# Eighteen weight pieces of a hybrid decoder block: the subtraction that splits them, on VectorE in place of GpSimd

## The chip, the core and the metric

The kernel runs on one core of a Trainium2 chip. The core's engines work side by side, each with its own queue of instructions in a fixed order: TensorE (PE, matrix products into PSUM), VectorE (DVE), ScalarE (ACT), GpSimd (POOL), and SyncE (SP), which here only starts DMAs. Instructions wait for one another by semaphores. The metric is the time of one execution on the device in microseconds (us), less is better.

## The reference, cut to what matters

One decoder layer on 512 tokens of width 1024. `u` is the normed input; one projection of `u` feeds a gated DeltaNet (GDN: short convolution, a triangular solve per chunk, a recurrence over chunks), a sparse attention (an indexer picks 128 keys per query) and two gates; then the output projection and a gated feed-forward with a short convolution.

```
proj = einsum("bsd,de->bse", u, w_in)          # q,k,v,z,a,b | dq,dk,dv | index q,k,w | gates a,b
gq, gk, gv = split(silu(causal_dwconv(g_qkv, gdn_conv_w)))      # gq, gk normed per head
T = triangular_solve(A + eye, eye)             # A[i,j] = beta_i (k_i . k_j) gamma_ij below the diagonal
u_, w = T @ (v * beta), T @ (k * beta * eG)
v_new = u_ - w @ state;  o = qg @ state + att @ v_new;  state = state * dlast + kd.T @ v_new
o_gdn = rmsnorm(o, gdn_norm_g) * silu(z)
score = sum_h iw[t,h] * relu(iq[t,h] . ik[s]) ; keep the top 128 causal keys ; softmax over them
m = sigmoid(gate_A) * o_gdn + sigmoid(gate_B) * o_dsa
h = h + m @ w_out ;  h = h + (silu(f_gate) * f_val) @ w_down ;  out = rmsnorm(h)
```

## The kernel before, in words

Every weight matrix is cut into pieces of 128 x 1024 numbers, in the order in which they are used. A piece is loaded from DRAM into a tile `raw`, ScalarE rounds it into its high part `whi` (line 198), and the low part `wlo = raw - whi` is a subtraction on an engine that the caller names (line 199, `piece(lo_engine)`). `raw`, `whi` and `wlo` have three buffers each. The activations are split in the same way (`uTh`, `uTl`; `xgh`, `xgl`). A product is then three matmuls (`passes`, lines 206 to 208): low times high, high times low, high times high, added up in a PSUM tile `acc`.

`channel_major` uses two pieces for two PSUM tiles of 128 channels by 512 tokens (48 matmuls of 512 columns); `token_major` uses two pieces for all tokens by 256 channels (96 matmuls of 256 columns). Which engine makes the low part of the first and of the second piece is their argument: `P` is GpSimd, `V` is VectorE.

The order of the work: the small projections; `uTh`/`uTl` (lines 421 to 425, one slice for each of eight blocks of 128 rows of `u`); the indexer's queries; then `gdn_half(0)` on heads 0 to 3: keys, queries and values (`conv_silu`, lines 463 to 469), the blocks `MT` of the solve's matrix (line 543), a round trip through DRAM, the solve itself on VectorE (lines 589 and 591, 30 steps of two dependent instructions with both inputs in SBUF), another round trip, transposes `UT` (line 601), the block inversion on TensorE (from line 607), and the recurrence over four chunks of 128 tokens (lines 637 to 665: `TR`, `upd`, `kS`). Beside it VectorE picks the top keys (lines 694 and 697) and the projections `dk` and `dq` are made (lines 701 to 709). Then `gdn_half(1)`, the attention (32 items, `attend_a` and `attend_b`), the gate projections `z`, `ga`, `gb` in 12 chunks, the mix, the output projection and the feed-forward.

This is the order in which the program is written. The order in which each engine's queue stands is made by a scheduler that runs over the whole program: it takes an instruction as soon as its model of the engines says that it is ready, by a priority that follows the written order, and pieces have their priority raised by 2000 places (line 196). So one stage's matmuls stand between another's small steps, and a change of one engine's work moves instructions on all engines.

Of the kernel before, what the change touches and what calls it, by code (L numbers as in the profile page):

```python
# [86 lines left out]
def hybrid_block(ctx: ExitStack, tc: tile.TileContext, x: bass.AP, xc: bass.AP, wp: bass.AP,  # L87
                 chan: bass.AP, rows: bass.AP, out: bass.AP):
    nc = tc.nc
    V, A, P, T = nc.vector, nc.scalar, nc.gpsimd, nc.tensor  # L90
# [5 lines left out]
    def acc(name="acc"):  # L96
        return psum.tile([128, 512], F, name=name, tag="acc", bufs=3)

    def tp(name="tp"):
        return psum.tile([128, 512], F, name=name, tag="tp", bufs=2)  # L100
# [4 lines left out]
    def rec(name="rec"):  # L105
        return psum.tile([128, 512], F, name=name, tag="rec", bufs=2)
# [87 lines left out]
    def piece(lo_engine):  # L194

        with tc.high_priority(offset=2000):
            raw, hi, lo = load()
            A.copy(hi, raw)  # L198
            lo_engine.tensor_sub(lo, raw, hi.bitcast(F))  # L199
        return hi, lo  # L200

    def passes(o, lhs, rhs, first, last, shared=False):


        (lh, ll), (rh, rl) = lhs, rhs
        a = T.matmul(o, lh, rl, start=first, stop=False, skip_group_check=shared)  # L206
        T.matmul(o, ll, rh, start=False, stop=False, skip_group_check=shared)  # L207
        return a, T.matmul(o, lh, rh, start=False, stop=last, skip_group_check=shared)  # L208

    def cols(pc, k, n, c0, c1):  # L210
        return tuple(w.rearrange("p (k c) -> p k c", c=n)[:, k, c0:c1] for w in pc)
# [81 lines left out]
    def u_blk(k, tb):  # L293
        return uTh[:, k, 128 * tb:128 * tb + 128], uTl[:, k, 128 * tb:128 * tb + 128]

    def token_major(eng):

        pcs = [piece(eng), piece(eng)]
        ps = [acc().rearrange("p (t c) -> p t c", c=256) for _ in range(2)]
        for i in range(2):  # L300
            for tb in range(NT):
                for k in range(4):
                    kk = 4 * i + k
                    passes(ps[tb // 2][:, tb % 2], u_blk(kk, tb), cols(pcs[i], k, 256, 0, 256),
                           kk == 0 and tb % 2 == 0, kk == KT - 1, shared=True)
        return ps

    def channel_major(eng, src=None, second=P):
        pcs = [piece(eng), piece(second)]
        ps = [acc(), acc()]  # L310
        for i, pc in enumerate(pcs):
            for t in range(2):
                for k in range(4):
                    kk = 4 * i + k
                    passes(ps[t], cols(pc, k, 256, 128 * t, 128 * t + 128),
                           src[kk] if src else (uTh[:, kk], uTl[:, kk]), kk == 0, kk == KT - 1)
        return ps
# [4 lines left out]
    def half_kb(name):  # L322
        return PR.tile([128, 512], F, name=name, tag="dqo", bufs=9)
# [119 lines left out]
    for b in range(1, NT):  # L443
        n = 128 * (b + 1)
        score[b] = mask[:, m_off[b]:m_off[b] + n]
        for h in range(H):
            p = tp("rel")[:, :n]
# [12 lines left out]
    def conv_silu(p, ti, dst=None):  # L460
        y = PR.tile([128, 512], F, name="y", bufs=2)
        t = PR.tile([128, 512], F, name="t", bufs=5)
        A.activation(y, p, AF.Identity, scale=cw[:, ti, 3:4])
        for s in range(1, 4):
            V.scalar_tensor_tensor(y[:, s:], p[:, :512 - s], cw[:, ti, 3 - s:4 - s], y[:, s:],  # L465
                                   op0=OP.mult, op1=OP.add)
        A.activation(t, y, AF.Tanh)
        dst = t if dst is None else dst
        V.scalar_tensor_tensor(dst, t, 1.0, y, op0=OP.add, op1=OP.mult)
        return dst  # L470
# [4 lines left out]
    def gdn_half(hh):  # L475
# [23 lines left out]


        for j in range(2):
            for t, p in enumerate(channel_major(P, second=V if hh else P)):
                conv_silu(p, 8 + HH * hh + 2 * j + t, kT[:, 2 * j + t])
        sumsq(kT, ssk, kt)
        V.tensor_scalar(ssk, ssk, EPS, None, op0=OP.add)
# [18 lines left out]
        for c in range(NT):  # L524
# [10 lines left out]
            for h2 in range(2):  # L535
                p = rec("kk").rearrange("p (h a i) -> p h a i", h=2, a=2)
# [145 lines left out]
        oA.append(at)  # L682

    gdn_half(0)


# [3 lines left out]
    for b in range(1, NT):  # L690
        n = 128 * (b + 1)
        top = const.tile([128, 8], F, name="top", bufs=2)
        for i in range(TOPK // 8):
            t = V.max(top, score[b])  # L694
# [4 lines left out]


    dk = PR.tile([128, 2, 512], F, name="dk", tag="k4", bufs=2)
    for t, p in enumerate(channel_major(P)):
        A.copy(dk[:, t], p)
    dq = []
    for j in range(4):
        for t, p in enumerate(channel_major(P)):
            q = half_kb("dq")
            A.copy(q, p)
            dq.append(q)

    gdn_half(1)

    oB = []
# [48 lines left out]
    def gate_bias(off):  # L762
        gb = PR.tile([128, 256], F, name="gbias", bufs=2)
        A.dma_start(gb, bcast(2048 + off, 256))
        return gb.unsqueeze(1).to_broadcast([128, 2, 256])

    def tmp(name):
        return PR.tile([128, 512], F, name=name, tag="t", bufs=5).rearrange("p (t c) -> p t c", c=256)

    def gated(o, p, bias):  # L770
        t = tmp("tg")
        V.tensor_add(t, p, bias)
        A.activation(t, t, AF.Tanh, scale=0.5)
        V.scalar_tensor_tensor(o, t, 1.0, o, op0=OP.add, op1=OP.mult)

    def z_chunk(j):
        for t2, p in enumerate(token_major(P)):
            t = tmp("tz")
            A.activation(t, p, AF.Tanh, scale=0.5)
            V.scalar_tensor_tensor(t, t, 1.0, p, op0=OP.add, op1=OP.mult)  # L780
            o = oAv[j][:, 2 * t2:2 * t2 + 2]
            P.tensor_mul(o, o, t)

    def ga_chunk(j):
        bias = gate_bias(256 * j)
        for t2, p in enumerate(token_major(P)):
            gated(oAv[j][:, 2 * t2:2 * t2 + 2], p, bias)

    def gb_chunk(j):
# [25 lines left out]
    for kind, j in _GATES:  # L815
        {"z": z_chunk, "ga": ga_chunk, "gb": gb_chunk}[kind](j)
        if kind == "gb" and j < 2:
            mix_chunk(j)
        if kind == "ga" and j >= 2:
            mix_chunk(j)  # L820
# [100 lines left out]
    for f in range(NF):  # L921
        e = P if f < 2 else V
# [124 lines left out]
```

## Time and profile before

| what | value |
|---|---|
| median of 3 runs (lowest, highest) | 950.55 us (949.44, 951.9) |
| the profiled execution: its time, and its span from first to last instruction | 950.98 us, 949.2 us |
| busy in the span: PE, DVE, ACT, POOL | 920.1, 601.7, 442.9, 193.3 us |
| mean granted TensorE clock | 0.988 |

The 1.8 us between span and time lie before the first and after the last instruction. A matmul's busy time overlaps the next one's, so a PE that is busy all the time can still be waiting for a moment; how dense its matmuls are is seen from how many start in a stretch. The granted clock has two levels, 1.2 and 2.4 GHz; a share of 1.00 means 2.4 GHz all through a stretch.

### The profile page before, as it was taken

Reading aid. Unit: us, or ns where it says so; the run is one execution under the profiler, and the core shown is the slowest. Engines: PE = TensorE matmul, PEld = TensorE weight load, DVE = VectorE, ACT = ScalarE, POOL = GpSimd, SP = SyncE. Lnnn points to the kernel's source line nnn. Section 1 sums busy time; section 2 is a strip of 40 time slices with the busy share of each in tenths; the row PEclk is TensorE's granted clock in tenths of the full one; section 3 lists DMA queues with packets and bytes.
Section 4 is the critical chain, followed back from the end, with each engine's and each line's share of the span. In section 5 each row is a group of like instructions: output and inputs, shape, how many; then the busy total and the mean of one; then the engine's idle time right before and its main releaser. Section 6 shows DMA issues by size and latency. Waiting matters only on the chain.

```text
span 949.2 us, 14678 instructions
## 1 busy us (share of the span) xinstructions
PE 920.1 (97%) x5671; PEld 807.0 (85%) x5671; DVE 601.7 (63%) x1222; ACT 442.9 (47%) x954; POOL 193.3 (20%) x131
## 2 busy tenths in 40 slices
PE   9989999979999998899999999999999999999997
PEld 8868877868888898899999999888888888888886
DVE  6885999889649769455634546666656665522424
ACT  7547754414559663355544435534444444422213
POOL 0264425411213352222243032000000000000201
PEclk9989999989999999999999999999999999999999
DMA  9323212432211232311422222323223332232212
GB/s 341 103 89 92 87 67 78 134 89 84 73 45 45 79 89 73 74 51 51 158 77 91 88 89 90 112 92 109 88 89 94 107 105 95 88 110 90 89 67 89
DMA packets 39830, 89.30 MB, mean 94 GB/s; under 512 B 15664, under 2 KB 16976, under 8 KB 39760
## 3 DMA queue, kind: packets, MB, share of 16 engines
q1 hardware_dynamic: 24192, 81.91, 25.9%
q10 hardware_dynamic: 15568, 6.45, 2.8%
q8 instruction: 45, 0.74, 0.3%
q14 instruction: 25, 0.20, 0.1%
HBM read 85.18 MB, written 3.16 MB: 93 GB/s over the span
## 4 chain that ended last, share of the span: by engine, by line
PE 72%; DVE 18%; DMA 3%; issue 2%; ACT 2%; POOL 1%; ACTq 0%; DVEq 0%; POOLq 0%
PE acc L206 19%; PE acc L207 18%; PE acc L208 18%; PE d L207 3%; PE d L208 3%; PE d L206 3%; DVE tw L589 2%; DVE wi L591 2%; DVE y L465 2%; PE lg L718 1%; DVE mask L697 1%; PE lg L736 1%; DMA MT<-bl 1%; DVE top L694 1%; DMA nn<-bl 1%
## 5 line engine op out<-in xcount | busy, mean ns | idle before, releaser
L198 ACT CAST whi<-raw 128x1024 fp32r<-128x1024 f32 x136 | 142.5, 1048 | 222.1 <-PE acc L208 102.3
L199 DVE TENSOR_TENSOR wlo<-raw,whi 128x1024 fp32r<-128x1024 f32 x80 | 99.7, 1247 | 158.8 <-ACT whi L198 158.6
L199 POOL TENSOR_TENSOR wlo<-raw,whi 128x1024 fp32r<-128x1024 f32 x56 | 139.0, 2484 | 294.4 <-ACT whi L198 260.3
L207 PE MATMUL acc<-hTh,wlo 128*128 128x512 f32 (+1 forms) x368 | 139.8, 380 | 0.0
L206 PE MATMUL acc<-hTl,whi 128*128 128x512 f32 (+1 forms) x368 | 139.1, 381 | 0.2 <-DVE hTl L845 0.2
L208 PE MATMUL acc<-hTh,whi 128*128 128x512 f32 (+1 forms) x368 | 138.8, 380 | 0.0
L206 PE MATMUL acc<-wlo,uTh 128*128 128x256 f32 x384 | 112.8, 294 | 1.1 <-DVE y L465 1.1
L206 PE MATMUL acc<-uTl,whi 128*128 128x512 f32 x272 | 109.5, 404 | 3.8 <-DVE uTl L425 3.6
L207 PE MATMUL acc<-whi,uTl 128*128 128x256 f32 x384 | 113.2, 295 | 0.0
L208 PE MATMUL acc<-whi,uTh 128*128 128x256 f32 x384 | 112.8, 294 | 0.0
L207 PE MATMUL acc<-uTh,wlo 128*128 128x512 f32 x272 | 108.7, 400 | 0.0
L208 PE MATMUL acc<-uTh,whi 128*128 128x512 f32 x272 | 108.2, 398 | 0.0
L206 PEld LDWEIGHTS acc<-hTl,whi 128*128 128x128 f32 x368 | 69.2, 188 | 13.4 <-DVE hTl L845 0.4
L207 PEld LDWEIGHTS acc<-hTh,wlo 128*128 128x128 f32 x368 | 69.2, 188 | 13.1
L208 PEld LDWEIGHTS acc<-hTh,whi 128*128 128x128 f32 x368 | 69.2, 188 | 13.1
L987 POOL TENSOR_TENSOR h<-h,gf 128x512 f32<-128x512 f32 (+1 forms) x8 | 10.6, 1349 | 338.6 <-ACT sq L983 338.6
L206 PEld LDWEIGHTS acc<-wlo,uTh 128*128 128x128 f32 x384 | 74.3, 194 | 2.8 <-DVE y L465 1.3
L207 PEld LDWEIGHTS acc<-whi,uTl 128*128 128x128 f32 x384 | 74.5, 194 | 1.6 <-issue 1.0
L208 PEld LDWEIGHTS acc<-whi,uTh 128*128 128x128 f32 x384 | 74.4, 194 | 1.6 <-issue 1.2
L904 DVE SCALAR_TENSOR_TENSOR fy<-acc,ch,fy 128x511 f32<-128x511 f32 x88 | 65.7, 747 | 11.0 <-ACT fy L902 9.5
L206 PEld LDWEIGHTS acc<-uTl,whi 128*128 128x128 f32 x272 | 52.1, 192 | 15.2 <-DVE uTl L425 4.7
L208 PEld LDWEIGHTS acc<-uTh,whi 128*128 128x128 f32 x272 | 52.1, 191 | 10.5
(310 smaller groups left out, 1891.1 us busy)
## 6 DMA issues: line engine op xcount, KB each, us to landing
raw<-in_wp_dram SPq DMA_DIRECT2D x137, 512.0 KB, 3.4
xT<-in_xc_dram SPq DMA_DIRECT2D x8, 256.0 KB, 5.2
xt<-in_x_dram SPq DMA_DIRECT2D x4, 512.0 KB, 8.4
ge<-gdr ACTq DMA_DIRECT2D x8, 256.0 KB, 3.2
h<-in_x_dram SPq DMA_DIRECT2D x4, 512.0 KB, 5.8
out_dram<-h SPq DMA_DIRECT2D x8, 256.0 KB, 2.3
raw<-in_wp_dram SPq DMA_DIRECT2D x4, 256.0 KB, 4.7
gbias<-in_rows_dram ACTq DMA_DIRECT2D x8, 128.0 KB, 3.1
```

Of the source, the lines that this page charges most:

```text
L198: A.copy(hi, raw)
L199: lo_engine.tensor_sub(lo, raw, hi.bitcast(F))
L206: a = T.matmul(o, lh, rl, start=first, stop=False, skip_group_check=shared)
L207: T.matmul(o, ll, rh, start=False, stop=False, skip_group_check=shared)
L208: return a, T.matmul(o, lh, rh, start=False, stop=last, skip_group_check=shared)
L465: V.scalar_tensor_tensor(y[:, s:], p[:, :512 - s], cw[:, ti, 3 - s:4 - s], y[:, s:], op0=OP.mult, op1=OP.add)
L589: V.tensor_mul(w, wi[:, 0:c, j:j + 1].to_broadcast([128, c, m]), nn[:, j:j + 1, j + 1:].to_broadcast([128, c, m]))
L591: tri.append(V.tensor_sub(wi[:, 0:c, j + 1:], wi[:, 0:c, j + 1:], w))
L694: t = V.max(top, score[b])
L697: V.match_replace(score[b], top, score[b], TAKEN)
L904: V.scalar_tensor_tensor(y[:, s:], p[:, :512 - s], fw[:, ti, 2 - s:3 - s], y[:, s:], op0=OP.mult, op1=OP.add)
L987: P.tensor_mul(hv, hv, gf[:, 512 * half + c.start:512 * half + c.stop])
```

## The change

The low parts of 18 pieces move from GpSimd to VectorE: four of the first half's keys, two of `dk`, six of the eight of `dq` (the second chunk's two stay), four of the first two `z` chunks and two of the first `ga` chunk. Of 56 pieces on GpSimd 38 are left, and of 80 on VectorE there are then 98. The arithmetic is the same.

```
         for j in range(2):
-            for t, p in enumerate(channel_major(P, second=V if hh else P)):
+            for t, p in enumerate(channel_major(P if hh else V, second=V)):
                 conv_silu(p, 8 + HH * hh + 2 * j + t, kT[:, 2 * j + t])
...
     dk = PR.tile([128, 2, 512], F, name="dk", tag="k4", bufs=2)
-    for t, p in enumerate(channel_major(P)):
+    for t, p in enumerate(channel_major(V, second=V)):
         A.copy(dk[:, t], p)
     dq = []
     for j in range(4):
-        for t, p in enumerate(channel_major(P)):
+        e = P if j == 1 else V
+        for t, p in enumerate(channel_major(e, second=e)):
...
     def z_chunk(j):
-        for t2, p in enumerate(token_major(P)):
+        for t2, p in enumerate(token_major(V if j < 2 else P)):
...
     def ga_chunk(j):
         bias = gate_bias(256 * j)
-        for t2, p in enumerate(token_major(P)):
+        for t2, p in enumerate(token_major(V if j == 0 else P)):
```

How the queues stand then is seen at three places. First VectorE while it builds the slices `uTl`: `wlo_831` and `wlo_903` are low parts of the first half's keys, `uv` and `uTl` the slices, `ikn` and `lnst` the indexer keys' norm, `iq` the indexer's queries. A plus is a row that is there only now, a minus one that stood there before.

```order
 L435 TENSOR_TENSOR iq_603<-acc_545,iq_603 64x512
 L352 TENSOR_TENSOR ikn_406<-ikn_406 128x4x64
+L199 TENSOR_TENSOR wlo_831<-raw_828,whi_830 128x1024
 L425 TENSOR_TENSOR uTl_86<-uv_516,uTh_85 128x512
 L423 SCALAR_TENSOR_TENSOR uv_524<-xT_124,ch_72,rB_178 128x512
 L425 TENSOR_TENSOR uTl_86<-uv_520,uTh_85 128x512
+L435 TENSOR_TENSOR iq_668<-acc_618,iq_668 64x512
 L345 TENSOR_REDUCE lnst_407<-ikn_406 128x4
 L423 SCALAR_TENSOR_TENSOR uv_528<-xT_125,ch_72,rB_178 128x512
-L435 TENSOR_TENSOR iq_668<-acc_618,iq_668 64x512
+L199 TENSOR_TENSOR wlo_903<-raw_900,whi_902 128x1024
 L425 TENSOR_TENSOR uTl_86<-uv_524,uTh_85 128x512
```

Three of the four key pieces (the third is `wlo_825`, a few rows earlier) now stand ahead of the last two slices.

Then TensorE where the block inversion of the first half begins: `m1` is its first matmul, which waits for `UT`; the `acc` rows around it belong to `dq` (`acc_2327`) and to the second half's keys (`acc_2401`, `acc_2402`). Before:

```order
L206 MATMUL acc_2327<-uTl_86,whi_2322 128x512
L207 MATMUL acc_2327<-uTh_85,wlo_2323 128x512
L607 MATMUL m1_1645<-UT_1639,MT_817 32x32
L208 MATMUL acc_2327<-uTh_85,whi_2322 128x512
L206 MATMUL acc_2327<-uTl_86,whi_2322 128x512
```

Now:

```order
L208 MATMUL acc_2402<-uTh_85,whi_2397 128x512
L206 MATMUL acc_2402<-uTl_86,whi_2397 128x512
L607 MATMUL m1_1645<-UT_1639,MT_817 32x32
L207 MATMUL acc_2402<-uTh_85,wlo_2398 128x512
L208 MATMUL acc_2402<-uTh_85,whi_2397 128x512
```

Forty-four matmuls of 512 columns that stood behind the first `m1` now stand ahead of it: 4 of `acc_2327`, 24 of `acc_2401`, 16 of `acc_2402`. They are missing between the second and the fourth chunk's `TR` of the recurrence, where 54 such matmuls stood and 9 stand now.

Last VectorE inside the first half's solve (lines 589 and 591; `wlo_2317` is a piece of `dq`, `mask` and `top` the choice of keys). Before:

```order
L589 TENSOR_TENSOR tw_1568<-wi_1567,nn_1564 128x75
L591 TENSOR_TENSOR wi_1567<-wi_1567,tw_1568 128x3x25
L589 TENSOR_TENSOR tw_1568<-wi_1567,nn_1564 128x96
L591 TENSOR_TENSOR wi_1567<-wi_1567,tw_1568 128x4x24
L589 TENSOR_TENSOR tw_1568<-wi_1567,nn_1564 128x92
```

Now:

```order
L591 TENSOR_TENSOR wi_1567<-wi_1567,tw_1568 128x3x25
L697 MATCH_REPLACE mask_393<-top_1983,mask_393 128x384
L589 TENSOR_TENSOR tw_1568<-wi_1567,nn_1564 128x96
L698 TENSOR_SCALAR mask_393<-mask_393 128x384
L591 TENSOR_TENSOR wi_1567<-wi_1567,tw_1568 128x4x24
L199 TENSOR_TENSOR wlo_2317<-raw_2314,whi_2316 128x1024
L589 TENSOR_TENSOR tw_1568<-wi_1567,nn_1564 128x92
```

Pieces and part of the choice of keys now stand between the steps of the solve; before, the last of the 384-wide choices stood ahead of it or at its first step.

## Rows read from the trace of the kernel before

**Rows 1.** Groups by line: instructions, then busy us, mean ns, idle before them.
```profile
L199 DVE TENSOR_TENSOR wlo<-raw,whi 128x1024 fp32r<-128x1024 f32 x80 | 99.7, 1247 | 158.8 <-ACT whi L198 158.6
L199 POOL TENSOR_TENSOR wlo<-raw,whi 128x1024 fp32r<-128x1024 f32 x56 | 139.0, 2484 | 294.4 <-ACT whi L198 260.3
```
**Rows 2.** PE's waits: who waited for whom, us in total, times, longest.
```profile
PE m L607 <- DVE UT L601: 8.1, 4, 3.8
PE pT L732 <- ACT pe L724: 3.8, 2, 2.6
PE acc L206 <- DVE uTl L425: 3.6, 2, 2.1
PE kk L539 <- DVE at L546: 1.8, 1, 1.8
```
**Rows 3.** Stretches: busy us (instructions) per engine, PEclk, DMA share, GB/s.
```profile
600.00:625.00 25.00, 25.00 (x112) 20.67 (x112) 14.88 (x18) 10.45 (x13) 0.00 (x0) 1.00 0.26 85
52.00:62.00 10.00, 7.57 (x22) 5.75 (x23) 9.51 (x24) 2.54 (x5) 5.74 (x12) 0.66 0.17 52
135.00:160.00 25.00, 22.36 (x121) 19.02 (x122) 24.93 (x65) 10.15 (x21) 10.55 (x9) 1.00 0.25 85
198.00:208.00 10.00, 4.79 (x74) 3.34 (x72) 7.05 (x13) 3.06 (x4) 4.21 (x2) 0.78 0.40 94
208.00:216.00 8.00, 8.00 (x84) 6.18 (x87) 7.66 (x16) 1.05 (x1) 0.00 (x0) 0.84 0.36 131
```
**Rows 4.** DVE in order of time, 36 to 64 us: start, us, instruction.
```profile
36.02 1.22 DVE L199 TENSOR_TENSOR wlo<-raw,whi 128x1024 fp32r<-128x1024 f32 x1
37.16 0.69 DVE L425 TENSOR_TENSOR uTl<-uv,uTh 128x512 fp32r<-128x512 f32 x1
37.76 2.39 DVE L350 TENSOR_SCALAR lnst<-lnst 128x4 f32<-128x4 f32 x1
...
54.56 0.17 DVE L136 TENSOR_SCALAR rik_it<-lnst 128x4 int32<-128x4 int32 x1
...
63.34 2.23 DVE L469 SCALAR_TENSOR_TENSOR kT<-t,y 128x512 f32<-128x512 f32 x1 [0.76 <-ACT t L467]
```
**Rows 5.** POOL in order of time, the first piece that it splits.
```profile
37.29 2.84 POOL L199 TENSOR_TENSOR wlo<-raw,whi 128x1024 fp32r<-128x1024 f32 x1 [13.51 <-DVE wlo L199]
```
**Rows 6.** PE in order of time, right behind its wait for the last slice.
```profile
55.99 0.63 PE L207 MATMUL acc<-uTh,wlo 128*128 128x512 f32 x1
56.42 0.63 PE L208 MATMUL acc<-uTh,whi 128*128 128x512 f32 x1
```
**Rows 7.** DVE in order of time, 130 to 177 us.
```profile
131.91 2.39 DVE L518 TENSOR_SCALAR ssq<-ssq 128x16 f32<-128x16 f32 x1
...
149.95 1.32 DVE L141 SCALAR_TENSOR_TENSOR rq_sc<-rq_sc 128x16 f32<-128x16 f32 x1
...
173.35 2.44 DVE L591 TENSOR_TENSOR wi<-wi,tw 128x56 f32<-128x56 f32 x1
...
176.07 0.22 DVE L591 TENSOR_TENSOR wi<-wi,tw 128x54 f32<-128x54 f32 x1
```
**Rows 8.** DVE in order of time, 295 to 347 us.
```profile
295.91 2.38 DVE L140 TENSOR_TENSOR ro_sc<-ro_sc,so 128x16 f32<-128x16 f32 x1
...
346.43 1.48 DVE L584 TENSOR_SCALAR wi<-nn 64x512 f32<-64x512 f32 x1 [3.25 <-DMA nn<-bl]
```
**Rows 9.** PE in order of time, where the first half's block inversion begins.
```profile
202.22 0.24 PE L607 MATMUL m<-UT,MT 32*32 32x32 f32 x2 [3.81 <-DVE UT L601]
...
206.07 1.91 PE L607 MATMUL m<-UT,MT 32*32 32x32 f32 x62 [1.40 <-DVE UT L601]
```
**Rows 10.** The chain that ended last, in order of time: start, us, what.
```profile
255.50 0.89 PE TR L646 x8
...
272.80 0.91 PE TR L646 x8
...
279.40 0.74 PE TR L646 x4
```

More of the change, by code (lines that the diff above doesn't have):

```diff
@@ L501, in gdn_half @@
         for j in range(2):
-            for t, p in enumerate(channel_major(P, second=V if hh else P)):
+            for t, p in enumerate(channel_major(P if hh else V, second=V)):
                 conv_silu(p, 8 + HH * hh + 2 * j + t, kT[:, 2 * j + t])
@@ L701, in hybrid_block @@
     dk = PR.tile([128, 2, 512], F, name="dk", tag="k4", bufs=2)
-    for t, p in enumerate(channel_major(P)):
+    for t, p in enumerate(channel_major(V, second=V)):
         A.copy(dk[:, t], p)
@@ L705, in hybrid_block @@
     for j in range(4):
-        for t, p in enumerate(channel_major(P)):
+        e = P if j == 1 else V
+        for t, p in enumerate(channel_major(e, second=e)):
             q = half_kb("dq")
@@ L776, in z_chunk @@
     def z_chunk(j):
-        for t2, p in enumerate(token_major(P)):
+        for t2, p in enumerate(token_major(V if j < 2 else P)):
             t = tmp("tz")
@@ L785, in ga_chunk @@
         bias = gate_bias(256 * j)
-        for t2, p in enumerate(token_major(P)):
+        for t2, p in enumerate(token_major(V if j == 0 else P)):
             gated(oAv[j][:, 2 * t2:2 * t2 + 2], p, bias)
```

## The prediction, made before the changed kernel ran

> **What bounds the kernel.** I read the stretches first. Where nothing else matters, as at 600 to 625 us, TensorE starts 112 matmuls of 512 columns in 25 us, 0.223 us each [rows 3]; there it sets the pace, and no other engine can shorten it. So the question is where it falls behind that pace. The list of TensorE's waits answers: 8.1 us for the transposes `UT` of the two solves, 3.8 us in the attention, 3.6 us for the slices `uTl`, 1.8 us for the blocks `at` [rows 2]. In three of these four the releaser is VectorE, and around them VectorE is full: 9.51 of 10 us at 52 to 62, 24.93 of 25 at 135 to 160 [rows 3]. Behind a wait the granted clock also falls to its lower level for a while: 0.66 on the mean of 52 to 62, 0.78 and 0.84 behind 198 [rows 3], and the matmuls then start 0.43 us apart [rows 6].
>
> So I looked at VectorE in order of time. A `TENSOR_SCALAR` on 128x4 numbers takes 0.17 us in one place and 2.39 in another [rows 4]. The long one runs from 37.76 to 40.15, and GpSimd's subtraction from 37.29 to 40.13 [rows 4, 5]: the small instruction ends when GpSimd's does. The same holds for two dependent steps of the solve, 2.44 us beside 0.22 [rows 7]. The trace so says that a low part on GpSimd (2.48 us, [rows 1]) can cost VectorE the rest of its length, if VectorE comes to an instruction that works from SBUF alone. Those that read PSUM are not held: beside the same pieces they keep their length.
>
> The Trainium skill, SBUF — State Buffer (Who interferes with whom), says that the two engines share one port pair, locked for a whole instruction when VectorE has two SBUF inputs or a two-port mode. The trace agrees, by the pair 2.44 and 0.22 us.
>
> **The change part by part.** A low part on VectorE occupies it from 36.02 to the next start at 37.16, 1.14 us [rows 4]; its mean of 1.25 us in the groups [rows 1] is longer because the end overlaps the next start, so I count 1.14. Eighteen of them are 20.5 us. Against that stand the holds that the same 18 pieces put on VectorE. I went through them in four sets.
>
> Keys, 4 pieces: four holds between 2.23 and 2.39 us [rows 4], less what these instructions take unheld (0.17, 0.4, 0.17 and 0.69 us): 7.8 us go, 4.6 come. `dk` and the first `dq`, 4 pieces: three holds, 2.39 the longest and 1.32 the shortest [rows 7], 4.9 us in excess, against 4.6. The other `dq`, 4 pieces, in the solve: three holds like the 2.44 [rows 7], 6.4 us against 4.6. `z` and `ga`, 6 pieces: four holds, the first 2.38 and the last 1.48 [rows 8], 6.3 us against 6.8. In sum 25.4 us go and 20.5 come. On VectorE alone that is little, but the sets do not weigh alike, and the queues are in another order. The terms, for TensorE:
>
> First term, the slices. Three of the moved pieces (3.4 us) stand ahead of the last two slices, and the three holds there (6.3 us) go. Ahead of the seventh slice two holds go (4.1 us) against three pieces: it comes 0.7 us sooner, and of the first wait, 1.5 us, 0.8 stays. The eighth comes 1.5 us sooner (6.3 less 3.4, less two `iq` subtractions of 0.7 that now precede it), and in TensorE's new order the seven matmul triples of the second `acc` that need no eighth slice go ahead of it, 7 x 3 x 0.223 = 4.7 us: the second wait, 2.1 us, goes. With it goes the low clock behind it, ten matmuls at 0.43 in place of 0.223 [rows 3, 6], 2.0 us. Sum -4.8; at best -5.6 (both waits), at worst -2.0 (only the wait for the eighth slice goes).
>
> Second term, 135 to 160. The 1.8 us for `at` [rows 2] arise because VectorE is full. It is relieved of 4.9 and loaded with 4.6, and it enters the stretch some us ahead. I take -1.5, between 0 and -1.8.
>
> Third term, the first half's block inversion. TensorE waits 3.81 and 1.40 us [rows 9]. In the new order 44 matmuls more stand ahead of it, 44 x 0.223 = 9.8 us. TensorE, 6.3 us ahead by the first two terms, so comes there 3.5 us later than its old arrival at 198.4, at 201.9. `UT` came at 202.2 and 206.1; up to it VectorE has 12 of the pieces, 13.7 us, and has lost 19.1 us of holds, so it should come up to 5 us sooner, at 197 to 201. Both waits go, 5.2 us, and the low clock behind them, 0.16 x 8 us at 208 to 216 and a little before, 1.5 us [rows 3]: -6.7. If `UT` comes no sooner, some 2.4 us of wait stay and the clock falls: -2.8.
>
> Fourth term, what pays for it: 45 matmuls that stood between the second and fourth `TR` of the recurrence are gone there, 10.0 us. The two steps took 23.9 us; the last one, with little between, took 6.6 us from `TR` to `TR` [rows 10]. Two such steps are 13.2 us, and 23.9 less 10.0 is 13.9, so the steps fill what is left almost exactly. I take +1.0; between 0 and +4 if a step needs 8.6 us.
>
> Fifth term, the second half. Its pieces are even on VectorE (6.8 against 6.3 us). TensorE's waits there, 2.9 us at the second block inversion (8.1 less 5.2) and 3.8 in the attention [rows 2, 9], have one help: TensorE has about 6 us more matmuls ahead of that inversion. I take -1.0, between -2.9 and +3. The pieces left on GpSimd in the second solve go on holding it.
>
> From 520 us on nothing changes. Sum: -4.8 - 1.5 - 6.7 + 1.0 - 1.0 = -13.0 us. The profiled execution took 950.98 us (span 949.2 and 1.8 around it), 0.4 above the median of 950.55, so 937.6 to 938.0; I say 938.
>
> **The rivals.** (a) The lead is given back. TensorE only runs ahead of the solve; the chain of the second half (its queries wait until the recurrence has freed `qT`, then blocks, solve, inversion) would have to come sooner by as much. If it comes only as much sooner as VectorE does, TensorE waits in 350 to 395 us for what it gained: then the first term and little more is left, 950.98 - 5.5, about 945. For it speaks that TensorE already waits there, 3.8 and 2.9 us; against it that the recurrence ran at TensorE's pace, not its own, 23.9 us where 13.2 are enough [rows 10].
>
> (b) VectorE becomes the bound, and the kernel slower. VectorE has no room from 100 to 200 us (24.93 of 25 [rows 3]). If a hold does not go with its piece, since GpSimd has other pieces there which then meet the next small step, the 12 pieces up to `UT` make it 13.7 us later. TensorE has 9.8 us more to do before it but is ahead by 4.8 at most, so it waits 13.7 - 9.8 + 4.8 + 5.2, and behind it the recurrence has no matmuls left to hide. The first half's chain then ends 13.7 us later, and what the slices gave, 4.8, and some 2.5 of the waits at its end go off: 957. It decides if less than 13.7 of the 19.1 us of holds go. A special form: `wlo_2317` and `wlo_2323` now stand behind steps of the solve, where TensorE needs them soon. Against it speaks that the holds in [rows 4, 7] are each covered by a moved piece; for it that two `dq` pieces and eight of queries and values stay on GpSimd in this part.
>
> The Trainium skill, Perfetto Trace Analysis (Optimizing Scalar/DVE Operations), speaks for this rival: when VectorE is saturated it would move work off it, even to GpSimd, though it adds that between those two it might not help. By that rule this change goes the wrong way. The trace bears out only the second half: VectorE is saturated, partly by waiting for GpSimd.
>
> (c) Gains and new waits cancel, or the scheduler's other order does as much harm as good: 950.
>
> **How the numbers follow.** The forecast, 938 with its own range of 930 to 945, has a chance of 0.60; (a) 945, from 942 to 947.5, 0.20; (b) 957, 0.12; (c) 950, 0.08. 0.3% is 2.9 us, about what a measurement of this kernel can tell from no change. Faster than that: 0.80; within: 0.08; slower: 0.12. All best ends together are 950.98 - 5.6 - 1.8 - 6.7 + 0 - 2.9 = 934; I let the range begin at 929, since an earlier recurrence may free more in the second half, whose own waits with their clock are some 8 us. Its upper end is 951: the worst ends, -2.0 + 0 - 2.8 + 4 + 3 = +2.2, take it to 953, but hardly all at once, and it takes in (a) and (c). About 0.2 is left out, most of it (b).
>
> **What would show it.** The first term: no wait of `acc` for `uTl` over 1 us and a clock of 1.00 at 52 to 62; `TENSOR_SCALAR` on `lnst` at 0.17 us. The third: no wait of `m` for `UT` in the first half, and 1.00 behind it. The fourth: from the second to the fourth `TR` about 14 us. The fifth: waits at 350 to 395 no longer than before; if they have grown by what the earlier stages gained, it was (a). In the solve, no step over 2 us but new steps of 1.14 us for the pieces. (b) would show as `UT` later than 206 us and a TensorE that waits for it longer than 5.2 us, or as waits for `wlo_2317`. I am wrong altogether if the holds remain in other places and VectorE's busy time rises by about 20 us in the first 205.

## The result and the profile after

The changed kernel takes 939.94 us in the median of its runs (936.59 to 942.07), the kernel before 951.22 beside it on the same chip: a ratio of 0.9876, 95% interval 0.9857 to 0.9896. It is faster by 1.24%, 11 to 12 us. The profiled execution took 938.66 us with a span of 936.5, 12.7 less than the 949.2 of before.

Part 1 of the page, then the groups of the low parts (counterparts of [rows 1]):

```profile
PE 914.4 (98%) x5671; PEld 802.7 (86%) x5671; DVE 603.3 (64%) x1240; ACT 442.0 (47%) x954; POOL 149.5 (16%) x113
...
L199 DVE TENSOR_TENSOR wlo<-raw,whi 128x1024 fp32r<-128x1024 f32 x98 | 121.5, 1240 | 158.2 <-ACT whi L198 158.1
...
L199 POOL TENSOR_TENSOR wlo<-raw,whi 128x1024 fp32r<-128x1024 f32 x38 | 91.2, 2399 | 238.3 <-ACT whi L198 223.9
```

The low parts' busy time on VectorE rose by 21.8 us (121.5 less 99.7), but all of VectorE's by only 1.6 (603.3 less 601.7): its other instructions take 20 us less. That is the first sign that holds went.

TensorE's waits (who waited for whom: us in total, times, longest), to be read against [rows 2]:

```profile
PE pT L733 <- ACT pe L725: 5.5, 5, 1.7
PE m L607 <- DVE UT L601: 2.7, 2, 1.8
PE lg L737 <- ACT pT L735: 1.6, 2, 0.8
PE wz L220 <- POOL ident masks.py:199: 1.4, 1, 1.4
PE kk L539 <- DVE at L546: 1.4, 1, 1.4
PE lg L719 <- ACT oB L741: 1.2, 3, 0.5
PE acc L206 <- DVE uTl L425: 1.0, 1, 1.0
```

`m` for `UT` fell from 8.1 to 2.7, `acc` for `uTl` from 3.6 to 1.0; the attention (`pT`) rose from 3.8 to 5.5. The four stretches of [rows 3] (busy us and instructions by engine, granted clock, DMA share, GB/s):

```profile
52.00:62.00 10.00, 10.00 (x43) 7.99 (x44) 9.15 (x24) 3.93 (x5) 3.98 (x8) 1.00 0.34 105
135.00:160.00 25.00, 23.39 (x128) 19.89 (x127) 25.00 (x63) 10.32 (x21) 9.80 (x7) 1.00 0.26 85
198.00:208.00 10.00, 7.26 (x79) 5.56 (x79) 6.42 (x13) 2.36 (x4) 2.40 (x1) 0.96 0.47 96
208.00:216.00 8.00, 8.00 (x40) 6.41 (x37) 7.87 (x15) 2.26 (x3) 2.39 (x1) 0.63 0.40 131
```

At 52 to 62 TensorE starts 43 matmuls where it started 22, and the clock stays at its upper level. Behind 198 the low level of the clock did not go; it moved, from 0.78 and 0.84 to 0.96 and 0.63. VectorE in order of time at the slices (counterparts of [rows 4]: start, us, instruction):

```profile
36.14 1.22 DVE L199 TENSOR_TENSOR wlo<-raw,whi 128x1024 fp32r<-128x1024 f32 x1
37.27 0.69 DVE L425 TENSOR_TENSOR uTl<-uv,uTh 128x512 fp32r<-128x512 f32 x1
37.88 0.16 DVE L350 TENSOR_SCALAR lnst<-lnst 128x4 f32<-128x4 f32 x1
...
39.31 1.22 DVE L199 TENSOR_TENSOR wlo<-raw,whi 128x1024 fp32r<-128x1024 f32 x1
...
51.76 0.21 DVE L354 TENSOR_SCALAR lnst<-lnst 128x4 f32<-128x4 f32 x1
...
63.74 0.68 DVE L469 SCALAR_TENSOR_TENSOR kT<-t,y 128x512 f32<-128x512 f32 x1
```

The same small step on `lnst` takes 0.16 us instead of 2.39, the `kT` at 63 us 0.68 instead of 2.23. Where a GpSimd piece is left, holds stay or appear (VectorE again, counterparts of [rows 7, 8]):

```profile
106.94 2.21 DVE L141 SCALAR_TENSOR_TENSOR rk_sc<-rk_sc,rk_it 128x16 f32<-128x16 f32 x1
...
142.94 2.05 DVE L140 TENSOR_TENSOR rq_sc<-rq_sc,ssq 128x16 f32<-128x16 f32 x1
...
149.85 2.36 DVE L140 TENSOR_TENSOR rq_sc<-rq_sc,ssq 128x16 f32<-128x16 f32 x1
...
183.56 2.37 DVE L589 TENSOR_TENSOR tw<-wi,nn 128x128 f32<-128x128 f32 x1
...
356.46 2.50 DVE L591 TENSOR_TENSOR wi<-wi,tw 128x126 f32<-128x126 f32 x1
```

TensorE where the first block inversion begins ([rows 9]), then the recurrence's `TR` in the chain that ended last ([rows 10]):

```profile
202.92 0.24 PE L607 MATMUL m<-UT,MT 32*32 32x32 f32 x2 [0.92 <-DVE UT L601]
...
206.81 1.70 PE L607 MATMUL m<-UT,MT 32*32 32x32 f32 x62 [1.82 <-DVE UT L601]
```

```profile
258.14 0.89 PE TR L646 x8
267.06 0.45 PE TR L646 x4
274.46 0.45 PE TR L646 x4
```

`UT` came 0.7 us later than before, not sooner (202.17 us in place of 201.46). TensorE's two waits halved all the same, 5.2 to 2.7 us, because TensorE itself came later. It got there at 202.00 (202.92 less the wait of 0.92) in place of 198.41, 3.6 us later, which is the 9.8 us of 44 more matmuls less a lead of 6.4 us that it had gained by then.

To see where the 12.7 us arose I summed, in each trace, every matmul's length at the upper clock in order of time, and compared the times at which the two sums are equal. This difference is called the lead below. The changed kernel is ahead by 4.9 us from 62 to 135, 6.4 at 180 to 198, and 12.8 from 400 us on, on the mean, to the end. In between the order of the matmuls differs, and the figure depends on the lengths taken for the small ones: 8 to 9 us at 230 to 282, 8 to 10 at 320 to 340.

The stretch of the second solve, before (the changed kernel's row stands below, under More pieces):

```profile
345.00:400.00 55.00, 48.35 (x494) 45.41 (x493) 41.33 (x106) 19.51 (x48) 16.84 (x8) 0.94 0.28 79
```

There the clock was at its lower level for a while; in the changed kernel it is 1.00.

### The profile page after: what moved, and what is told of

It reads as the page before. It is cut to its first block, busy times and chain, and to the rows that moved or that the text cites. A ratio compares the mean times of both kernels' runs of the same rounds, so it can differ in the third digit from the quotient of the medians.

```text
span 936.5 us, 14668 instructions
## 1 busy us (share of the span) xinstructions
PE 914.4 (98%) x5671; PEld 802.7 (86%) x5671; DVE 603.3 (64%) x1240; ACT 442.0 (47%) x954; POOL 149.5 (16%) x113
## 4 chain that ended last, share of the span: by engine, by line
PE 76%; DVE 16%; DMA 3%; ACT 3%; issue 2%; ACTq 0%; POOL 0%; DVEq 0%; POOLq 0%
PE acc L206 19%; PE acc L208 19%; PE acc L207 19%; PE d L207 3%; PE d L208 3%; PE d L206 3%; DVE wi L591 2%; DVE tw L589 2%; PE lg L737 2%; DVE mask L697 1%; PE lg L719 1%; DVE wlo L199 1%; DVE top L694 1%; DMA nn<-bl 1%; DVE y L465 1%
## 5 line engine op out<-in xcount | busy, mean ns | idle before, releaser
L198 ACT CAST whi<-raw 128x1024 fp32r<-128x1024 f32 x136 | 142.7, 1049 | 224.6 <-PE acc L208 121.5
L199 DVE TENSOR_TENSOR wlo<-raw,whi 128x1024 fp32r<-128x1024 f32 x98 | 121.5, 1240 | 158.2 <-ACT whi L198 158.1
L199 POOL TENSOR_TENSOR wlo<-raw,whi 128x1024 fp32r<-128x1024 f32 x38 | 91.2, 2399 | 238.3 <-ACT whi L198 223.9
L206 PEld LDWEIGHTS acc<-hTl,whi 128*128 128x128 f32 x368 | 69.2, 188 | 13.4 <-DVE hTl L846 0.4
L208 PEld LDWEIGHTS acc<-hTh,whi 128*128 128x128 f32 x368 | 69.2, 188 | 13.2
```

## The experiments

All times are medians on a chip with the kernel before beside them (951.74 us for the first four, 952.61 for the next four, 951.26 for the last four); ratios are to that. 0.001 of the ratio is 0.95 us. Three theories stand against each other: VectorE's holds (a VectorE instruction is held when it can't end before a GpSimd low part does, so that the low part costs VectorE the rest of its length), VectorE's load (each piece moved costs what it takes there), and the order (the scheduler's new queues alone).

**The parts alone.** First the keys:

```
-  for t, p in enumerate(channel_major(P, second=V if hh else P)):      # keys
+  for t, p in enumerate(channel_major(P if hh else V, second=V)):
```

> Only the four low parts of the first half's keys go to VectorE; the other 14 stay on GpSimd. Holds theory (VectorE loses the rest of a GpSimd low part whenever it comes to an instruction on SBUF alone, and the keys' four holds stood ahead of the slices uTl): the first term alone, clock 1.00 and no second wait at 52 to 62, lead of 4.9 us at 62 as in the changed kernel, kept to the end: 945 to 946. Rival, lead given back: the solve's end does not come sooner by this, so TensorE waits there for what it gained: 949 to 951 with the longest wait for UT 3 to 5 us longer than before. Rival, order alone: the gain sits in how the scheduler placed the whole, a part gives another order and any time from 938 to 955.

Measured: 948.09 us, 0.997 [0.9953, 0.9988]. The list of waits of this kernel, its row on `UT`, and then three stretches:

```profile
PE m L607 <- DVE UT L601: 6.2, 2, 5.8
```

```profile
52.00:62.00 10.00, 9.65 (x41) 7.73 (x42) 9.10 (x25) 3.94 (x5) 3.91 (x9) 1.00 0.32 105
135.00:160.00 25.00, 22.90 (x116) 19.33 (x115) 24.90 (x67) 10.90 (x21) 11.01 (x8) 0.93 0.20 64
208.00:216.00 8.00, 8.00 (x77) 6.13 (x77) 7.62 (x16) 1.04 (x1) 1.42 (x1) 0.50 0.37 123
```

The first stretch is nearly the changed kernel's, and the lead at 62 us was some 4.5. But at 160 to 198 only 1.0 was left (116 matmuls at 135 to 160 and a clock of 0.93, against 121 and 1.00 before), and then it was gone: `UT` came at 206.1 us, 4.6 later than before, and TensorE waited 5.8 for it. In this execution the lead of the slices was given back whole; that is rival (a). But it was 3.6 us over its kernel's median, and by the ratio of all twelve runs 2.9 us (1.1 to 4.5) of the lead were kept. So the time lies between the two forecasts, 945 to 946 and 949 to 951, and how much of the lead the keys keep alone stays open. Then `dk` and `dq`:

```
-  for t, p in enumerate(channel_major(P)):            # dk
+  for t, p in enumerate(channel_major(V, second=V)):
-      for t, p in enumerate(channel_major(P)):        # dq
+      e = P if j == 1 else V
+      for t, p in enumerate(channel_major(e, second=e)):
```

> Only the two low parts of dk and six of dq go to VectorE. Holds theory: the slices are as before (second wait of 2.1 us and low clock at 52 to 62 stay); what the changed kernel gained from 135 to 290 us, 1.5 and about 3.6 us, comes: 945 to 947, if it does not rest on the keys' lead. Rival, the sets lean on each other: without the keys' lead TensorE comes later to the solve and finds UT ready, so the waits for UT vanish without this set too and only 1 to 2 us are left: 948 to 950. Rival, VectorE as the bound: 8 x 1.14 = 9.1 us more on VectorE ahead of UT, which comes later, 953 or more.

Measured: 946.78 us, 0.9949 [0.9932, 0.9966], within the first theory's span. That is an agreement of the number alone: in the profiled execution (949.96 us, 3.2 over the median) `UT` came at 207.98, 6.5 later than before, with 566 matmuls ahead of it and a wait of 2.9 us. And the gates:

```
-  for t2, p in enumerate(token_major(P)):             # z
+  for t2, p in enumerate(token_major(V if j < 2 else P)):
-  for t2, p in enumerate(token_major(P)):             # ga
+  for t2, p in enumerate(token_major(V if j == 0 else P)):
```

> Only the six low parts of z and ga go to VectorE. Prediction's own working: even on VectorE, 6.8 us come and 6.3 us of holds go, so 949 to 951. Rival: the 3 us that the changed kernel gained from 340 to 400 us (no wait of m for UT there, no low clock) came from this set, whose GpSimd pieces stood in the second half: 947 to 948, with the second solve's wait for UT, 2.85 us before, gone.

Measured: 945.27 us, 0.9936 [0.9917, 0.9955]: the largest part of the three, where the expectation had at most 2 us. The lead was 0.4 us until 120, 3.1 at 160 to 198, 0.4 again at 230 to 300 (TensorE waited 5.7 us for the first `UT`), and 5.7 from 400 on, so what stayed arose in the second half. The waits for the second `UT` were still 2.0 us, so the rival's account of how is not borne out either. The three parts add up to 0.0145, the whole change gave 0.0124; within the intervals the parts are additive.

**Neither, and both.** To take the work of the 18 pieces apart from their holds, one kernel leaves their subtraction out, and one does it on both engines:

```
-  lo_engine.tensor_sub(lo, raw, hi.bitcast(F))
+  if lo_engine is None:          # the 18 pieces
+      return hi, hi
```

> As the changed kernel, but the 18 low parts are made on no engine: their matmuls take the high part in place of the low one (the output's last digits change by that). Holds theory: the holds were the price and VectorE's own 1.14 us a piece cost little, since 25.4 us of holds went for 20.5 us of work: TensorE is left with the waits of the changed kernel where VectorE is full (1.0 for the slices, 1.4 for at, 2.7 for UT with some 1.5 us of low clock), of which most goes: 932 to 937. Rival, VectorE's load as such is what TensorE waits for: 20.5 us less load, of which 13.7 stand ahead of UT, give as much again as the change gave: 925 to 931. Rival, order: no lower than the changed kernel, 938 to 942, since no wait of the first 200 us rests on VectorE any more.

```
+  if lo_engine == "both":        # the 18 pieces
+      V.tensor_sub(lo, raw, hi.bitcast(F))
+      P.tensor_sub(raw, raw, hi.bitcast(F))
```

> The changed kernel, but behind VectorE's low part of each of the 18 pieces GpSimd does the same subtraction once more, into raw, which nobody reads any more. So TensorE gets the low parts from VectorE as in the changed kernel, and GpSimd's 18 instructions are there as before. Holds theory: the holds come back on top of VectorE's own work, as in 951.7 for GpSimd alone, 931.1 for neither, about 940 for VectorE alone: 931.1 + 20.6 + 8.8 = 960, between 953 and 965, with VectorE's busy time up by some 20 us against the changed kernel. Rival, latency: what GpSimd's low parts cost was that they were done 1.3 us and a queue later than VectorE's, and TensorE waited for them: 938 to 942. Rival, order of the queues alone: 938 to 945, since TensorE's order is nearly the changed kernel's.

Measured: neither 931.13 us, 0.9787 [0.9765, 0.9809]; both 957.09, 0.5% over before, 1.0052 [1.0033, 1.0071]. In the first, the matmuls read the high part where the low one stood, so its products are other ones altogether, not only in their last digits; TensorE starts the same number of matmuls. Its time lies between the spans of the holds theory (932 to 937) and of the load (925 to 931), and does not decide between them. The second excludes latency and order as the whole cause: there TensorE gets its low parts from VectorE as in the changed kernel, and 18 instructions whose result nobody reads cost 0.0176, 17 us, while VectorE's busy time rises by 23 us (603.3 to 626.5). These instructions also keep each `raw` longer, but no wait of TensorE in that kernel is for a load, and only one, of 1.8 us, for a low part of VectorE. How they cost it is seen on GpSimd and on VectorE of that kernel:

```profile
51.23 2.35 POOL L201 TENSOR_TENSOR raw<-raw,whi 128x1024 f32<-128x1024 f32 x1
57.09 2.37 POOL L201 TENSOR_TENSOR raw<-raw,whi 128x1024 f32<-128x1024 f32 x1
```

```profile
51.74 2.38 DVE L427 SCALAR_TENSOR_TENSOR uv<-xT,ch,rB 128x512 f32<-128x512 f32 x1
...
57.55 2.47 DVE L429 TENSOR_TENSOR uTl<-uv,uTh 128x512 fp32r<-128x512 f32 x1
```

`uv` takes 0.75 us and `uTl` 0.69 unheld. Between these two TensorE waits for the slice that comes off at 55.94:

```profile
55.99 0.51 PE L210 MATMUL acc<-uTl,whi 128*128 128x512 f32 x1 [4.20 <-DVE uTl L429]
```

In the changed kernel the only wait for a slice is 1.03. The four kernels make a table. Its last column counts, from each trace, the `acc` matmuls on the slices `uTh` and `uTl` that TensorE starts ahead of the first `m` of the inversion.

| the 18 low parts on | ratio | first `UT` starts, us | matmuls ahead of `m` |
|---|---|---|---|
| no engine | 0.9787 | 186.50 | 524 |
| VectorE (the change) | 0.9876 | 202.17 | 568 |
| GpSimd (before) | 1 | 201.46 | 524 |
| both | 1.0052 | 217.38 | 571 |

```profile
186.50 0.70 DVE L603 STREAM_TRANSPOSE UT<-MT 32x512 f32<-32x512 f32 x1 [0.81 <-DMA MT<-bl]
```

```profile
202.17 0.70 DVE L601 STREAM_TRANSPOSE UT<-MT 32x512 f32<-32x512 f32 x1 [1.52 <-DMA MT<-bl]
```

```profile
217.38 0.70 DVE L605 STREAM_TRANSPOSE UT<-MT 32x512 f32<-32x512 f32 x1 [0.90 <-DMA MT<-bl]
```

On either engine the pieces make `UT` 15 to 16 us later, and on both 31. So up to `UT` holds and work weigh the same. But for the whole kernel they don't: the pieces on GpSimd cost 0.0213 (20 us, 1.1 a piece), on VectorE 0.0089 (8.5 us, 0.5 a piece). Where the difference arises is seen when, in the profiled executions, TensorE's waits (those over 0.15 us) are added up with the time that the lower clock cost it (length of a stretch times what its clock's share lacks to 1), in us:

| the 18 low parts on | to 66 us | from 66 to the first inversion | next 34 us | the rest | sum | span less sum |
|---|---|---|---|---|---|---|
| no engine | 2.2 | 0.0 | 4.9 | 8.6 | 15.7 | 916.4 |
| VectorE | 2.5 | 1.6 | 6.2 | 9.7 | 19.9 | 916.6 |
| GpSimd | 8.4 | 3.1 | 8.6 | 13.2 | 33.3 | 916.0 |
| both | 8.2 | 7.9 | 6.0 | 11.3 | 33.4 | 919.3 |

In the first three kernels the rest of the span is the same to 0.6 us, so these waits and the clock are what tells them apart. The largest difference between GpSimd and VectorE is at the slices, 5.9 us, where holds fall on the steps that TensorE waits for. At the first inversion it is 2.4, and there the count of matmuls comes in. With the pieces on VectorE the queue has 44 matmuls more ahead of the inversion, 9.8 us. Had there been 524, TensorE would have come there at 192.0 by the lead of 6.4 and waited some 10 us: an estimate, but by it the 44 matmuls kept the lead that had been gained before. With the pieces on GpSimd the queue has as many as with no pieces at all, which fits an order made as if they cost VectorE nothing. No run changes the order and leaves the rest, so this part is argued from the counts. With both, the queue has the changed kernel's order nearly (97 of 100 matmuls in the same sequence). The holds that come on top cost TensorE 5.7 us at the slices and 6.3 from there to the inversion; at the inversion itself, where `UT` is 15.2 us later, they cost nothing more, since TensorE comes later too.

**More pieces.** The second chunk of `dq`, the second half's first key pieces, and six more gate pieces, each added to the changed kernel:

```
-  e = P if j == 1 else V
+  e = V
```

> The changed kernel with the two pieces of dq's second chunk on VectorE too. They hold VectorE at 142.94 and 149.85 us, 1.9 and 2.2 us beyond the instructions' own 0.17; against that come 2 x 1.14. Holds theory: 1.8 us less on VectorE ahead of the blocks at (wait 1.4) and of UT (2.7): 0.3 to 0.997 of... in time, 938 to 939.5, 1 to 2 us below the changed kernel's 939.9. Rival, the load rule (VectorE is full there and each piece costs it 1.14 us whatever GpSimd does): 941 to 943.

```
-  for t, p in enumerate(channel_major(P if hh else V, second=V)):
+  for t, p in enumerate(channel_major(V, second=V)):
```

> The changed kernel with the first pieces of the second half's two key chunks on VectorE. One of them holds the first half's solve at 183.56 us by 2.08 us. Holds theory: UT comes 0.9 us sooner at most, so the waits for UT (2.7 us) fall to about 1.8, and the low clock behind them (207 to 214) stays: 938.5 to 940. If the order puts more matmuls ahead of the inversion and the clock stays up: 937. Rival, load: 940 to 942.

```
-  token_major(V if j == 0 else P)     # ga
+  token_major(V if j < 2 else P)
-  token_major(P)                      # gb
+  token_major(V if j < 2 else P)
```

> The changed kernel with six more gate pieces (second ga, first two gb chunks) on VectorE. In the changed kernel four of them hold the second solve at 346.89, 356.46, 364.95 and 372.39 us, 8.5 us in all, and two later ones 0.5. 6.8 us come. Moving the first six z and ga pieces alone gave 6.1 us (0.9936), all behind 290 us, though VectorE gained nothing in sum; what counts is then that the solve's own steps are not held. Holds theory: the second UT comes some 4 us sooner, TensorE's waits for the attention and the blocks at 345 to 400 (6 us) go in part: 935 to 938. Rival, even on VectorE and so even in time: 939 to 941. Rival, VectorE late for the attention's and the gates' own steps: 942 to 944.

Measured: 934.04 us, 0.981 [0.9791, 0.9829]; 936.53, 0.9833 [0.9814, 0.9852]; 930.26, 0.9768 [0.9747, 0.9789]. All three are faster than the changed kernel's 0.9876, and each by more than VectorE's own balance gave. Each also came out below the holds theory's span, so no theory foresaw the sizes. (For the keys an aside in the expectation gave 937, if more matmuls stand ahead of the inversion and the clock stays up: 574 stand ahead, and no wait for the first `UT` is left.) With `dq`'s second chunk, TensorE behind 198 us:

```profile
198.00:208.00 10.00, 10.00 (x102) 7.87 (x100) 9.52 (x18) 3.27 (x4) 2.39 (x1) 1.00 0.50 107
208.00:216.00 8.00, 5.71 (x27) 4.70 (x26) 7.91 (x15) 2.66 (x4) 0.00 (x0) 1.00 0.18 66
```

The wait for `UT` and the low clock behind it are both gone (mean clock of the span 0.999), though `UT` came at 203.5, later still: TensorE has other matmuls there. With the gates, the stretch of the second solve, first in the changed kernel, then in this one:

```profile
345.00:400.00 55.00, 48.58 (x528) 44.83 (x528) 45.14 (x111) 19.88 (x42) 16.10 (x8) 1.00 0.27 73
```

```profile
345.00:400.00 55.00, 53.63 (x565) 50.92 (x564) 44.41 (x126) 22.65 (x48) 4.62 (x4) 1.00 0.29 85
```

VectorE is as busy with the pieces as it was with the holds (44.41 and 45.14), TensorE is busy for 5.0 us more, and in its list of waits the attention's falls:

```profile
PE pT L733 <- ACT pe L725: 1.4, 2, 0.7
```

It was 5.5 us. The second `UT` did not come sooner (383.6 against 382.5 us), against my expectation; the waits that went were others. Then all that is left of the first half's queries and values, and combinations:

```
-  channel_major(P, second=V if hh else P)     # queries, values
+  channel_major(P if hh else V, second=V)
```

> The changed kernel with the eight low parts of the first half's queries and values on VectorE, where it is full (25 of 25 us at 135 to 160). In the changed kernel these eight hold VectorE by 1.72, 0.34, 0.56 and 2.05 us, 4.7 in all; 8 x 1.14 = 9.1 us come. Counted by holds against work: VectorE is 4.4 us later at the blocks at and at UT, and TensorE waits more there: 942 to 945. Rival, price by piece (a low part costs the whole kernel 1.14 us on GpSimd and 0.49 on VectorE, by the kernel that left the 18 out): 8 x 0.65 = 5 us less, 934 to 936.

Measured: 937.65 us, 0.9856 [0.9825, 0.9886], not told apart from the changed kernel. Neither way of counting met it: 4.4 us of balance against it on VectorE cost nothing, and a price by the piece would have given 5 us. Next, `dq`'s second chunk and the six gates together; then these and the keys:

> The changed kernel with the second chunk of dq (2 pieces) and six more gate pieces (second ga, first two gb) on VectorE. Apart they gave 0.9810 and 0.9768 of before, the changed kernel 0.9876. Holds theory: the first clears the first half's inversion, the other the second solve, two stretches, so they add up: 0.9768 - (0.9876 - 0.9810) = 0.970, 922 to 926. Rival, what the first half gains the second gives back: no better than the gates alone, 929 to 931.

> As the kernel with dq's second chunk and six more gates, and the first pieces of the second half's two key chunks on VectorE too. Holds theory: both of these clear the same wait for UT of the first half (each alone left none), so the second adds nothing or at most the hold of 2.08 us in the solve: 0.968 to 0.971, 921 to 926. Rival, each piece gives its own: 0.970 - (0.9876 - 0.9833) = 0.9657, 918 to 920. Rival, load: 1.1 us a piece, 926 to 928.

Measured: 926.98 us, 0.9744 [0.9713, 0.9775], and 928.35, 0.9757 [0.9725, 0.979]. The first adds up less than fully: the 0.970 expected lies just below the interval, though within what the intervals of its terms leave open. In the second the keys add nothing that can be told from noise, which fits that both clear the same wait; but the time lies outside the 921 to 926 that this gave, next to the load rival's 926 to 928. At last no low part on GpSimd at all:

```
-  lo_engine.tensor_sub(lo, raw, hi.bitcast(F))
+  V.tensor_sub(lo, raw, hi.bitcast(F))
```

> The changed kernel with all 38 low parts that are left on GpSimd on VectorE. By holds: dq's second chunk, the key pieces and six gates give 15 us as far as the runs show, the eight of queries and values cost up to 4, and those from 383 us on, where TensorE waits for nobody, give and cost nothing: 924 to 930, no better than the kernel with eight moved. Rival, price by piece: 38 x 0.65 = 25 us less than the changed kernel, 913 to 917. Rival, VectorE as the bound, 38 x 1.14 = 43 us more on it: above 935.

Measured: 926.61 us, 0.974 [0.971, 0.977], the same as with eight pieces more than in the changed kernel, and within the first span. Thirty further pieces, 34 us of work on VectorE, cost nothing and gave nothing. These two versions, some 2.6% below before, beat the kernel before and the changed one.

## Why the prediction was right, and where it was not

The sum was -13.0 us and the spans differ by 12.7. That holds on VectorE are the price was right. The size is right in part by luck, because two errors cancel: the third and fourth terms gave some 3 to 4 us less than said, the fifth 2.5 to 3.7 us more.

First term, the slices: -4.8 said, 4.9 us of lead found at 62 us. The wait that was to stay at 0.8 is 1.0, the second is gone, the clock is 1.00, 21 more matmuls start. All its steps held. What it left out is that this lead had to survive the first inversion: with the keys alone the profiled execution lost it there and just before, and in the changed kernel it lasted.

Second term, 135 to 160: -1.5 said, 1.5 found (lead 4.9 to 6.4; 128 matmuls in place of 121, 7 x 0.223 = 1.6). But not as said: the wait of `kk` for `at` fell only from 1.8 to 1.4, and the rest came from a wait for the choice of keys, `rel` for `mask`, which the sum did not have (1.3 to 0.2).

Third term, the block inversion: -6.7 said. The step that failed is that `UT` comes up to 5 us sooner since 19.1 us of holds go for 13.7 of work. `UT` came 0.7 us later. Summing over VectorE's instructions that overlap one of GpSimd's what they took beyond the lower quartile of their shape, I find 24.2 us of holds ahead of `UT` before and 12.2 after: 12.0 went. Of the 19.1 some seven found another place; three holds that make up 6.2 of them stand above, two at 142.94 and 149.85 us from the `dq` pieces that stayed, one at 183.56 from a key piece of the second half, a solve step this time. For the four keys alone the same sum falls by 1.7 where I had 7.8. And the work was larger, 13 more low parts ahead of `UT` (17 in place of 4), 14.8 us. This is the first half of rival (b), that a hold need not go with its piece. Its second half, that TensorE then waits longer, did not follow. The bound that I had given for `UT` no sooner, -2.8, is what came: 2.5 us of waits gone (5.2 to 2.7), the low clock still there.

Fourth term, the recurrence: about 14 us said from the second to the fourth `TR`, 16.3 found (258.14 to 274.46), against 23.9 before. The 2.4 us beyond the 13.9 are not the recurrence's own: 22 more matmuls of 128 columns, at some 0.11 us, stand in that stretch now. So it cost about nothing where I had +1.0. Third and fourth together gave about 2 us (at the fourth `TR` the changed kernel is 5.1 us earlier with 3.0 us of matmuls more behind it, a lead of 8.1) where I had 5.7.

Fifth term, the second half: -1.0 said, -3.5 (by the waits and the clock) to -4.7 found (lead 8.1 to 12.8), beyond its best end of -2.9. The error is in its argument, that pieces even on VectorE are even in time. The gates alone gave 6.1 us in a balance of 6.3 against 6.8. VectorE is not full there (41.33 of 55 us at 345 to 400 before), so a piece can find a gap, while a hold falls on a step of the norms or of the solve, which others wait for. The wait for the second `UT`, 2.9 us, went whole; the attention's waits took back some 4. What the sum had at nothing is the low clock behind that wait: before, a share of 0.94 at 345 to 400, which is 3.3 us lost, and 1.00 now.

The rivals: (a), the lead given back, is what the profiled execution of the keys alone shows; in the whole change the lead grew. (b) began and did not decide. (c) is excluded by the interval.

One reading of the prediction was too wide. It had every VectorE instruction that works from SBUF alone held. Transposes, maxima and steps on one number per partition do so too, and keep their length beside a piece (the last section has the numbers).

What decided, then, was not when `UT` comes. Up to the inversion the gain is 6.4 us, mainly holds that went where TensorE waits for VectorE: with 18 dead subtractions on top (both) the waits and the clock cost 8.2 us at the slices again, in nearly the same order of matmuls. At the inversion the order kept it. From the changed kernel on, with 18 to 56 pieces moved, `UT` starts at 202 to 204 us whatever moves; but ahead of the first `m` stand 524 matmuls before, 568 in the changed kernel, 588 with `dq`'s second chunk and 593 with all pieces moved, and the waits for `UT` go from 5.2 us by 2.7 to nothing. The prediction had the 44 matmuls only as a later arrival of TensorE, beside a `UT` that comes sooner; without that they alone had to cover the wait. Whether the second half gained in the same way is open: with six more gate pieces its `UT` did not come sooner either, and no count of this kind was made there, since attention, gates and recurrence all mix in it.

The Trainium skill, Perfetto Trace Analysis (Optimizing Scalar/DVE Operations), would move work off a saturated VectorE, even to GpSimd, though it adds that between these two it might not help. The runs bear out the addition: here the opposite paid, 0.9876 with 18 pieces moved to VectorE and 0.9744 with 26, and the thirty beyond these cost nothing (0.974).

## What to carry to other kernels

Before giving an elementwise operation to a second engine, look at what the first one does meanwhile: small instructions with a duration far over their neighbours of the same shape, which end when the other engine's do, are the price, and it is paid on a dependent chain. What a delay costs depends on what the waiting engine still has to do: pieces that made `UT` 15 to 16 us later on either engine cost 8.5 us on VectorE and 20 on GpSimd, the largest part of the difference (5.9 of the 13.4 us in the traces) where the holds fell directly ahead of TensorE's inputs. So look for holds there first, and count the work that stands ahead of a wait. And expect holds to move when only some of the pieces move: what is left on the second engine meets the next small step.

## What the runs showed of the hardware

A hold needs nothing but GpSimd at work on SBUF: 18 subtractions whose results nobody reads made VectorE's instructions of 0.7 us last 2.4. Not every VectorE instruction is held. Held were, under a piece that had begun, those with two tensors from SBUF as inputs (a step of the solve took 2.44 us in place of 0.22) and `TENSOR_SCALAR` on 128x4 and 128x16 numbers (2.39 in place of 0.17). Instructions that take one of their inputs from PSUM keep their length (`y` from `acc`, 0.75 us beside a piece at 65.90 in the kernel before, 0.74 elsewhere), and so do some with one SBUF input: `MATCH_REPLACE8` (0.54 us at 153.31 in the kernel before, while the `rq_sc` step behind it at 153.77, under the same piece, took 1.88), `MAX8`, the transposes of `UT` (0.70 at 205.31), and steps on one number per partition (0.15). The clock's lower level appeared behind some waits of TensorE and not behind others: in the changed kernel it came with two waits of 0.92 and 1.82 us at the first inversion, and not with the attention's waits of up to 1.7 us (1.00 all through 345 to 400); before, the same stretch with the second inversion's wait had 0.94.
